# Compression's activation at high priority, a second raw tile loaded ahead, one more sample unit outside the own tiles, and a transpose one output tile later

## The chip, the cores and the metric

The kernel runs on one core of a Trainium2 chip. A core has five engines that work side by side, each through its own queue in order: TensorE (PE: matrix products and transposes; PEld is its weight load), VectorE (DVE), ScalarE (ACT: activation functions, copies), GpSimd (POOL) and SyncE (SP, which here issues DMAs). The metric is the device time of one execution in microseconds. The kernel before took 1641.71 us as the median of three runs (1640.44 to 1644.45).

## The reference

One layer of a decoder trunk for two groups of requests that share the weights: a prompt of 1024 tokens, and eight sample sequences of eight new tokens with 4096 cached ones. In short:

```python
h = rms_norm(x, norm1) * (1 + scale1) + shift1
z = h @ w_in
(q, kc, vc, ks, vs, kw, vw, gates, conv_bg, conv_cg, conv_h, pool_in) = jnp.split(z, IN_SPLITS, axis=-1)
...
k_cmp = rms_norm(compress(full[:, :, 0], cmp_pe[0], cmp_w1[0], cmp_w2[0]), k_gain[0])
v_cmp = compress(full[:, :, 1], cmp_pe[1], cmp_w1[1], cmp_w2[1])
o_cmp, p_cmp = cmp_attention(q, k_cmp, v_cmp, q_pos)
top_i, sel_ok = select_blocks(p_cmp, q_pos, -(-full.shape[1] // SLC_BLOCK))
o_slc = slc_attention(q, top_i, sel_ok, q_pos, full[:, :, 2], full[:, :, 3])
...
o_attn = (g[..., 0:1] * o_cmp + g[..., 1:2] * o_slc + g[..., 2:3] * o_win).reshape(B, T, ATTN_W)
...
x = x + gate1 * (jnp.concatenate([o_attn, y_conv, y_pool], axis=-1) @ w_out)
h = rms_norm(x, norm2) * (1 + scale2) + shift2
x = x + gate2 * swiglu(h, w_up, w_down)
```

The compression, which two of the four edits touch, is this; `raw` is the cache of the raw keys or values of a sequence, read page by page through a page table:

```python
blk = raw[:, idx] + pe[:, None, :]
...
return jax.nn.silu(flat @ w1) @ w2
```

`idx` takes blocks of 32 positions every 16 positions. All data are float32.

## The kernel before

The layer is computed in stages, one after the other, and within a stage several generators ("the attention of the prompt", "the compression", and so on) are run interleaved. Each generator yields the time at which its next step is ready by a planner's own clock (`self.t`, advanced by `self.use`), and the planner takes a ready step. Behind the planner the framework's scheduler orders the instructions on each engine by a priority, that is by their place in the program unless `high_priority(offset=AHEAD)` moves them 2000 places ahead, and by a simulated time at which they are ready. A small edit can therefore move instructions in a whole stage.

The stages on the profile's time: normalisation and input projection up to about 364 us; the attention stage up to about 811; the output projection; then the feed-forward part up to the end.

*Compression.* Each of the eight sample sequences has four raw tiles, numbered 0 to 31 over all, of 128 partitions by 8 pages of 256 numbers. `compress_load(i)` takes a tile from the pool `stream` (three buffers, one of which holds the weights w1 through the stage) and gathers its eight pages with eight DMAs of 128 KB: six on SP's queue and two on POOL's (L533). In `compress`, PE multiplies a tile by w1 in 16 products (`stream` as the input, two rows of the trace for each). Once its products are issued, tile i + 2 is loaded. Two tiles are evacuated together by ACT and DVE (L586 to L590) into `pair` tiles. When a sequence's four tiles are done, `compress_post` adds two of these (L623, DVE), applies Silu (L625, ACT, with a load of its function table), and multiplies by w2 (`pair,c_w` on PE), then normalises. The next sequence may not start its evacuation before `compress_post` has released the pair tiles.

The first EARLY = 3 sequences are compressed during the input projection, with one tile more, number 12, loaded ahead. `compress_more` then compresses the prompt's own keys, for which `compress_prompt` borrows a stream tile. The remaining tiles, 12 to 31, belong to the attention stage. There, before the change, tile 14 went into the buffer that `compress_prompt` had left, and tile 13 into that of tile 12, after its products.

*Prompt attention.* For eight blocks j of queries and two halves h there are two units each, with the selected and compressed keys ("slc") and with the window's ("win"). A unit is: scores on PE as sums of three products of a high and a low part (`kh,qh`, `kl,qh`, `kh,ql`), mask and maximum on DVE (L1136), exponential on ACT (L1148), the scale on DVE (L1150 to L1154) and POOL (L1158), transposes of the probabilities on PE (`ident,P`, L145), their evacuation (`pt`), and the products with the values (`pt,vt`, `pt,vcp`).

*Sample attention.* 36 units, nine for each pair of sequences. Each loads a tile of 1 MB, and does scores (`unit,qb` or `stream,qb`), the exponential (`e`, L1408), four transposes (`ident,e`), their evacuation (`spt`, L163 or L165) and the products with the values (`unit,spt`) into `part`. `sample_load` gives a unit a tile: two tiles `unit` belong to the sample attention alone, and once all the compression is done the three stream tiles join them, but only for units with a number below LATE_UNITS:

```python
fit = [x for x in self.unit_free if self.unit_next < LATE_UNITS or x == "unit"]
```

A pair of sequences ends with `sample_combine`, a chain on DVE (L1458) that weighs eleven parts into `co`. The last pair's `co` is transposed and stored by `sample_store(3)`, which stands in the output projection.

*Output projection.* For each quarter c of the tokens and each of eight output tiles m: 24 products (`mh,w_hi`, `mh,w_lo`, `ml,w_hi`), then the residual (L1517). `mh` and `w_hi` are the high parts of the mixed activations and of the weights, made by ACT at L177, `ml` and `w_lo` the low parts by DVE at L173. The last `sample_store` is issued after the products of c = 0, m = 2.

Of the kernel before, what the change touches and what calls it, by code (L numbers as in the profile page):

```python
# [11 lines left out]
AF = mybir.ActivationFunctionType  # L12
OP = mybir.AluOpType
# [29 lines left out]
AHEAD = 2000  # L43
EARLY = 3
PACE = 0.5
LATE_UNITS = 33
PINNED = ("q3",)
EPS = 1e-6

# [15 lines left out]
class Kernel:  # L65
# [508 lines left out]

    def compress_more(self):
        yield from self.compress_prompt(self.cp)
        self.octets = 0

    def compress_evac(self, uv, vt, pre, half, n=16):
# [40 lines left out]

    def compress_post(self, pool, b, vt, pre, r, w=256):
        nc = self.nc
        nc.vector.tensor_tensor(pre[:, :, 0:w - 1], pre[:, :, 0:w - 1], vt[:, :, 1:w], op=OP.add)  # L623
        r = self.use("dve", 0.1 + w * 0.0023, r)
        nc.scalar.activation(vt[:, :, 0:w], pre[:, :, 0:w], AF.Silu, bias=self.pec[:, 0:1])  # L625
        r = self.use("act", 0.2 + w * 0.002, r, table="silu") + 0.2
        if b is None:
            nc.vector.memset(vt[:, :, w - 1:w], 0.0)
# [17 lines left out]
        r = self.use("act", 0.55, self.t["pe"])  # L646
# [3 lines left out]
        m = yield from self.bank_of(self.cmp_tags[0])  # L650
# [13 lines left out]
        r = self.use("act", 0.4, self.t["pe"], table="sqrt")  # L664
# [3 lines left out]
        r = self.use("dve", 0.1 + w * 0.0077, r)  # L668
# [679 lines left out]
    def sample_load(self, pool):  # L1348
# [4 lines left out]
        while self.unit_next < 36:  # L1353
            fit = [x for x in self.unit_free if self.unit_next < LATE_UNITS or x == "unit"]
            if not fit:
# [193 lines left out]
    def output_projection(self, wp, pool, nt, x1, opened):  # L1549
        nc = self.nc  # L1550
# [57 lines left out]
        for cs in groups:  # L1608
            ss = {c: nt.tile([P, HALF], F32, name="n_ss", bufs=2) for c in cs}
            for m in range(KT):  # L1610
                w = ws.pop(0)
                load()
                for c in cs:
# [7 lines left out]
                    else:  # L1621
                        for k in range(KT):
                            done = self.mm3(acc[:, :HALF], wk[k], parts[c, k][:2], k == 0, k == KT - 1)
                    if c == 0 and m == 2:
                        with self.tc.issue_after(done.ins):
                            self.sample_store(3, self.bank(), self.co, self.smo)
                    if c == cs[-1]:
# [2 lines left out]
                    r = self.residual(xv, acc[:, :HALF], m, c * HALF, HALF, self.mod[:, 2], xv, nt)  # L1630
                    nc.sync.dma_start(self.x1_d[:, m, c * HALF:c * HALF + HALF], xv)
                    r = self.square_sum(nt, ss[c], xv, m, HALF, r, HALF, None)
# [771 lines left out]
```

## Time and profile before

| what | us |
|---|---|
| median of three runs | 1641.71 |
| the profiled execution | 1639.42 |
| its span | 1637.8 |
| PE busy, share of the span | 1557.0, 95% |
| DVE / ACT / POOL busy | 1084.8 / 783.2 / 694.1 |
| PE idle from 364 to 437 us | 16.0 |
| PE idle from 437 to 800 us | 19.6 |
| PE idle from 800 to 828 us | 7.8 |

Times in the profile count from the span's start. A row of a timeline has the start, the length, the engine, the line of the kernel, the operation and its output and inputs by the names of the tiles; "x32" is a count of rows drawn together. What stands in brackets is the time for which the engine was idle just before, and what ended it. In the trace a product of float32 shows as two rows, in the order of the program as one.

### The profile page before, as it was taken

What the parts mean: (1) busy time and instruction counts of PE and PEld (TensorE: products, weight loads), DVE (VectorE), ACT (ScalarE), POOL (GpSimd) and SP (SyncE); (2) the same over time, 40 slices, a digit from 0 to 9 for tenths busy, and PEclk for the clock granted to TensorE, in tenths of its full rate; (3) what the DMA queues carried; (4) which work ended last, traced back from release to release, by engine and by line L of the source; (5) the groups of instructions that cost most, each with busy time, mean ns of one, the idle gap of its engine ahead of it and who ended that gap; (6) DMA issues with size and microseconds to landing.
All of it is one profiled execution on the core that took longest, in us unless ns stands there. A gap on an engine that the chain in (4) does not pass through costs nothing. (4 is left out here: it accounts for less than half of the span.)

```text
span 1637.8 us, 35584 instructions
## 1 busy us (share of the span) xinstructions
PE 1557.0 (95%) x12569; PEld 1378.3 (84%) x12569; DVE 1084.8 (66%) x2660; ACT 783.2 (48%) x1852; POOL 694.1 (42%) x848
## 2 busy tenths in 40 slices
PE   6999999996999999998899999999999999899998
PEld 2899997895777665655599999999999999899998
DVE  4823224895565678765689878777777775577768
ACT  3522215445676766756666534333433443344444
POOL 3231010265243223323213357554554444788765
PEclk9999999997999999999999999999999999999999
DMA  9585665555566475243396864446343445967643
GB/s 341 193 289 173 190 200 156 146 174 167 164 191 184 141 211 156 85 134 107 137 313 217 289 226 177 147 166 212 134 148 136 146 147 198 374 236 253 215 159 126
DMA packets 198020, 309.47 MB, mean 189 GB/s; under 512 B 26513, under 2 KB 132306, under 8 KB 197522
## 3 DMA queue, kind: packets, MB, share of 16 engines
q1 hardware_dynamic: 175346, 268.50, 49.7%
q0 software_dynamic: 9568, 28.40, 5.3%
q10 hardware_dynamic: 12928, 10.29, 2.1%
q8 instruction: 100, 1.64, 0.4%
q14 instruction: 78, 0.64, 0.1%
HBM read 237.10 MB, written 74.20 MB: 190 GB/s over the span
## 5 line engine op out<-in xcount | busy, mean ns | idle before, releaser
L141 PE MATMUL bank<-b_lo,w_hi 128*128 128x272 f32 x1232 | 352.7, 288 | 1.0 <-DVE b_lo L173 1.0
L141 PE MATMUL bank<-b_hi,w_hi 128*128 128x272 f32 x1232 | 350.5, 289 | 2.6 <-ACT f_m L1752 1.2
L141 PE MATMUL bank<-b_hi,w_lo 128*128 128x272 f32 x1232 | 347.3, 288 | 0.0
L141 PEld LDWEIGHTS bank<-b_hi,w_hi 128*128 128x128 f32 x1232 | 229.8, 188 | 5.1 <-ACT f_m L1752 3.0
L141 PEld LDWEIGHTS bank<-b_lo,w_hi 128*128 128x128 f32 x1232 | 231.6, 188 | 2.0 <-DVE b_lo L173 1.9
L141 PEld LDWEIGHTS bank<-b_hi,w_lo 128*128 128x128 f32 x1232 | 229.5, 188 | 0.0
L1158 POOL TENSOR_SCALAR P<-P,st 128x128 f32<-128x128 f32 (+10 forms) x192 | 108.6, 580 | 229.0 <-DVE st L1154 152.0
L173 DVE TENSOR_TENSOR w_lo<-w_raw,w_hi 128x512 fp32r<-128x512 f32 (+2 forms) x118 | 113.6, 972 | 78.7 <-ACT w_hi L177 78.1
L173 POOL TENSOR_TENSOR w_s<-w_raw 128x512 f32<-128x512 f32 (+1 forms) x84 | 119.9, 1428 | 61.9 <-DVE w_lo L173 42.2
L141 PEld LDWEIGHTS bank<-stream 128*128 128x128 f32 x1056 | 125.8, 196 | 17.3 <-issue 10.5
L177 ACT ACTIVATE w_hi<-w_raw 128x512 fp32r<-128x512 f32 (+2 forms) x120 | 79.5, 678 | 125.9 <-PE bank L141 80.2
L141 PE MATMUL bank<-stream 128*128 128x128 f32 x1056 | 132.0, 282 | 6.3 <-DMA stream<-in_cacheA 6.2
L1148 ACT ACTIVATE P<-P,st 128x128 f32<-128x128 f32 (+10 forms) x192 | 112.7, 588 | 52.4 <-DVE st L1136 33.5
L173 POOL TENSOR_TENSOR x<-x,d_m 128x272 f32<-128x272 f32 x136 | 117.5, 886 | 32.7 <-DVE x L1952 18.6
L141 PE MATMUL bank<-h_hi,w_hi 128*128 128x384 f32 (+1 forms) x384 | 130.7, 340 | 0.5 <-DVE q L769 0.5
L141 PE MATMUL bank<-g,w_hi 128*128 128x272 f32 x616 | 121.7, 293 | 6.6 <-DVE x L1952 6.6
L141 PE MATMUL bank<-h_hi,w_lo 128*128 128x384 f32 (+1 forms) x384 | 126.2, 329 | 0.0
L141 PE MATMUL bank<-h_lo,w_hi 128*128 128x384 f32 (+1 forms) x384 | 125.6, 327 | 0.0
L173 DVE TENSOR_TENSOR w_lo<-w_s,w_hi 128x512 fp32r<-128x512 f32 (+1 forms) x119 | 112.4, 946 | 16.8 <-ACT w_hi L177 14.4
L141 PE MATMUL bank<-g,d_hi 128*128 128x272 f32 x616 | 119.0, 289 | 1.3 <-DVE x L1955 1.3
L1779 POOL TENSOR_TENSOR pair<-pair,f_v 128x272 f32<-128x272 f32 x44 | 44.9, 1021 | 174.2 <-DVE f_v L1749 132.4
L1952 DVE SCALAR_TENSOR_TENSOR x<-bank,mod,x 128x272 f32<-128x272 f32 (+1 forms) x200 | 90.4, 476 | 41.2 <-PE bank L141 28.5
(381 smaller groups left out, 3826.6 us busy)
## 6 DMA issues: line engine op xcount, KB each, us to landing
g<-g_d SPq DMA_DIRECT2D x63, 544.0 KB, 6.2
g_d<-f_s SPq DMA_DIRECT2D x57, 544.0 KB, 3.4
wada<-in_wada SPq DMA_DIRECT2D x96, 256.0 KB, 5.4
stream<-in_cacheA SPq DMA_DIRECT2D x192, 128.0 KB, 3.2
unit<-in_cacheB SPq DMA_DIRECT2D x152, 128.0 KB, 2.3
w_raw<-in_wup SPq DMA_DIRECT2D x38, 512.0 KB, 4.3
stream<-in_cacheB SPq DMA_DIRECT2D x104, 128.0 KB, 2.2
w_raw<-in_wout SPq DMA_DIRECT2D x24, 512.0 KB, 5.6
```

The costliest lines, as they stand in the source:

```text
L141: return self.nc.tensor.matmul(out, lhsT, rhs, start=start, stop=stop, skip_group_check=chain)
L173: (self.nc.vector if eng == "dve" else self.nc.gpsimd).tensor_tensor(out, a, b, op=op)
L177: self.last_hi = self.nc.scalar.activation(hi, src, AF.Copy)
L1148: nc.scalar.activation(Ps, Ps, AF.Exp, scale=-1.0, bias=sy[:, g, 0:1], accum_out=sy[:, g, 1:2])
L1158: nc.gpsimd.tensor_scalar(Ps, Ps, sy[:, g, 3:4], 0.0, op0=OP.mult, op1=OP.add)
L1779: nc.gpsimd.tensor_tensor(g[:, 1], s1, v, op=OP.mult)
L1952: self.last_gate = nc.vector.scalar_tensor_tensor(out[:, :n], acc[:, :n], self.mod[:, 5, m, 0:1], out[:, :n], op0=OP.mult, op1=OP.add)
```

## The change

Four edits:

- `compress_more` loads tile 13 (EARLY * 4 + 1) once `compress_prompt` is through.
- In `compress_post` the addition and the Silu stand under `high_priority`.
- LATE_UNITS is 34 and not 33, so that unit 33 may take a stream tile, and only units 34 and 35 are bound to the two tiles `unit`.
- The last `sample_store` is issued after the products of m = 3 and not m = 2.

```diff
-LATE_UNITS = 33
+LATE_UNITS = 34
...
     def compress_more(self):
         yield from self.compress_prompt(self.cp)
+        self.compress_load(EARLY * 4 + 1)
         self.octets = 0
...
     def compress_post(self, pool, b, vt, pre, r, w=256):
         nc = self.nc
-        nc.vector.tensor_tensor(pre[:, :, 0:w - 1], pre[:, :, 0:w - 1], vt[:, :, 1:w], op=OP.add)
-        r = self.use("dve", 0.1 + w * 0.0023, r)
-        nc.scalar.activation(vt[:, :, 0:w], pre[:, :, 0:w], AF.Silu, bias=self.pec[:, 0:1])
+        with self.tc.high_priority(offset=AHEAD):
+            nc.vector.tensor_tensor(pre[:, :, 0:w - 1], pre[:, :, 0:w - 1], vt[:, :, 1:w], op=OP.add)
+            r = self.use("dve", 0.1 + w * 0.0023, r)
+            nc.scalar.activation(vt[:, :, 0:w], pre[:, :, 0:w], AF.Silu, bias=self.pec[:, 0:1])
         r = self.use("act", 0.2 + w * 0.002, r, table="silu") + 0.2
...
-                    if c == 0 and m == 2:
+                    if c == 0 and m == 3:
                         with self.tc.issue_after(done.ins):
                             self.sample_store(3, self.bank(), self.co, self.smo)
```

The order on the engines changes through the whole attention stage. Three places follow. In these rows the number is the row's place on its engine, then come the line, the operation with its tiles, its shape and a count; numbers behind a tile's name only tell its copies apart.

The first is PE at the start of the attention stage, where `stream` is a raw tile of the compression and `kh`, `kl` are the keys of the first prompt unit. Before:

```order
1477 L141 MATMUL bank<-h_sq,mean_h 128x320
1478 L141 MATMUL bank<-stream 128x128 x16
1479 L141 MATMUL bank<-kh_3584,qh 128x192 x4
1480 L141 MATMUL bank<-kh_3586,qh 128x128
1481 L141 MATMUL bank<-kl_3585,qh 128x192 x2
1482 L141 MATMUL bank<-kh_3584,ql 128x192 x2
1483 L141 MATMUL bank<-kl_3585,qh 128x192 x2
1484 L141 MATMUL bank<-kh_3584,ql 128x192 x2
1485 L141 MATMUL bank<-stream 128x128 x14
```

After:

```order
1477 L141 MATMUL bank<-h_sq,mean_h 128x320
1478 L141 MATMUL bank<-stream 128x128 x48
1479 L141 MATMUL bank<-kh_3611,qh 128x192 x2
1480 L141 MATMUL bank<-kl_3612,qh 128x192 x2
1481 L141 MATMUL bank<-kh_3611,ql 128x192 x2
1482 L141 MATMUL bank<-kh_3611,qh 128x192 x2
1483 L141 MATMUL bank<-kl_3612,qh 128x192 x2
1484 L141 MATMUL bank<-kh_3611,ql 128x192 x2
1485 L141 MATMUL bank<-kh_3613,qh 128x128
1486 L141 MATMUL bank<-stream 128x128 x16
```

Before, tile 12 was followed by scores and then by tile 13; now the three tiles 12, 13 and 14 stand in a row, and the scores behind them.

The second is PE in block j = 3, first half, from the last scores with the selected keys to the first transposes of their probabilities (`ident,P`). Before:

```order
1665 L141 MATMUL bank<-kh_3584,ql 128x256 x2
1666 L141 MATMUL bank<-unit,qb 64x512 x2
1667 L145 MATMUL bank<-ident,P 128x64
1668 L141 MATMUL bank<-pt,vt__291 64x256 x4
1669 L145 MATMUL bank<-ident,P 128x64 x7
1670 L141 MATMUL bank<-pair_5299,c_w_82 64x256 x2
1671 L145 MATMUL bank<-ident,e 128x128 x4
1672 L141 MATMUL bank<-stream 128x128 x16
1673 L141 MATMUL bank<-pt,vt__291 64x256 x2
1674 L141 MATMUL bank<-pair_5966,mean_h 128x256
1675 L145 MATMUL bank<-ident,pair_5966 128x128 x2
1676 L145 MATMUL bank<-ident,P 128x64 x32
```

The eight `ident,P` of rows 1667 and 1669 belong to an earlier unit; row 1676 is this unit's. After:

```order
1677 L141 MATMUL bank<-kh_3611,ql 128x256 x2
1678 L141 MATMUL bank<-stream 128x128 x7
1679 L141 MATMUL bank<-unit,spt 64x128 x8
1680 L141 MATMUL bank<-kh_3613,qh 128x512 x2
1681 L141 MATMUL bank<-kl_3614,qh 128x512 x2
1682 L141 MATMUL bank<-kh_3613,ql 128x512 x2
1683 L141 MATMUL bank<-kh_3613,qh 128x512 x2
1684 L141 MATMUL bank<-kl_3614,qh 128x512 x2
1685 L141 MATMUL bank<-kh_3613,ql 128x512 x2
1686 L145 MATMUL bank<-ident,P 128x64 x16
```

A whole raw tile stood between the scores and the transposes; now it is seven products of one, a sample unit's products with its values, and the scores of the window unit.

The third is the end of the attention stage, where `unit,qb`, `ident,e` and `unit,spt` are sample unit 35 and `mh,w_hi` begins the output projection. PE before:

```order
2163 L145 MATMUL bank<-ident,P 63x128 x3
2164 L141 MATMUL bank<-unit,spt 64x128 x8
2165 L141 MATMUL bank<-pt,vt__291 64x256 x2
2166 L141 MATMUL bank<-pt,vcp 64x256 x2
2167 L141 MATMUL bank<-unit,qb 64x512 x2
2168 L145 MATMUL bank<-ident,e 128x128 x4
2169 L141 MATMUL bank<-unit,spt 64x128 x8
```

PE after:

```order
2173 L141 MATMUL bank<-unit,qb 64x512 x2
2174 L141 MATMUL bank<-pt,vt__291 64x256 x2
2175 L141 MATMUL bank<-pt,vcp 64x256 x2
2176 L145 MATMUL bank<-ident,e 128x128 x4
2177 L141 MATMUL bank<-unit,spt 64x128 x8
```

ACT at the same place, from unit 35's exponential (L1408, after the change L1410) to the copy of its transposes, `spt`. Before:

```order
628 L1408 ACTIVATE e,den<-e,nm 128x512
629 L177 ACTIVATE mh<-pair_6564 128x272 x2
630 L177 ACTIVATE mh<-pair_6566 128x272
631 L1447 ACTIVATE cw<-nm,cs 128x2
632 L177 ACTIVATE mh<-pair_6566 128x272
633 L177 ACTIVATE mh<-pair_6568 128x272 x2
634 L177 ACTIVATE mh<-pair_6570 128x272 x2
635 L177 ACTIVATE w_hi<-w_raw 128x512 x2
636 L163 ACTIVATE spt<-bank 128x512
```

After:

```order
619 L1410 ACTIVATE e,den<-e,nm 128x512
620 L177 ACTIVATE mh<-pair_6613 128x272 x2
621 L1230 ACTIVATE mo<-bank 128x256
622 L1449 ACTIVATE cw<-nm,cs 128x2
623 L177 ACTIVATE mh<-pair_6615 128x272 x2
624 L177 ACTIVATE mh<-pair_6617 128x272 x2
625 L177 ACTIVATE mh<-pair_6619 128x272 x2
626 L163 ACTIVATE spt<-bank 128x512
```

On PE, unit 35's scores moved ahead of the last products with the values; on ACT, one copy `mo` stands ahead of `spt` where two `w_hi` stood. The first `part` copy behind `spt` (L163), which stood behind four `w_hi` and six `mh`, now stands behind six `w_hi`.

## The prediction, made before the changed kernel was run

> **What bounds the kernel now.** I read the head of the profile first: busy time of each engine, then the chain that ended last.
>
> ```profile
> span 1637.8 us, 35584 instructions
> PE 1557.0 (95%) x12569; PEld 1378.3 (84%) x12569; DVE 1084.8 (66%) x2660; ACT 783.2 (48%) x1852; POOL 694.1 (42%) x848
> PE 9%; DVE 1%; issue 0%; POOL 0%; ACT 0%; DVEq 0%
> ```
>
> TensorE (PE) works 95% of the span, no other engine over 66%, and the chain is PE's nearly throughout. So this change can win or lose only the time in which PE is idle, or runs at a lower granted clock, in the stretches it reorders. The program's matmuls are the same before and after; only their order differs. The windows by stage say how much idle time there is:
>
> ```profile
> 364.00:437.00 73.00, 57.01 (x468) 46.33 (x466) 42.95 (x204) 39.49 (x131) 35.35 (x84) 0.86 0.58 174
> 437.00:800.00 363.00, 343.37 (x3514) 234.35 (x3516) 234.30 (x985) 239.64 (x629) 109.95 (x182) 0.97 0.49 142
> 800.00:828.00 28.00, 20.20 (x156) 17.03 (x153) 20.12 (x54) 17.15 (x41) 5.01 (x6) 0.94 0.69 243
> 870.00:1638.00 768.00, 748.37 (x5897) 743.01 (x5897) 567.63 (x1022) 328.76 (x736) 445.04 (x431) 0.99 0.56 194
> ```
>
> Columns: start:end, length, busy time (and instructions) of PE, PEld, DVE, ACT and POOL, then the granted clock of PE, DMA share and GB/s. The start of the attention stage (364 to 437) holds 73.00 - 57.01 = 16.0 us of idle PE and a granted clock of 0.86; its middle (437 to 800) 19.6 us; its last units and the first output tiles (800 to 828) 7.8 us. Behind 870 PE is busy and nothing there is touched in kind: whatever is won up to 828 moves the rest earlier, one for one. Two rows of PE's waits in the stage (364 to 870), grouped by what it waited for (total, times, longest), are used below; the waits with a place of their own are shown in the timelines:
>
> ```profile
> PE bank L141 <- ACT kh L177: 1.5, 2, 1.0
> PE bank L145 <- POOL P L1158: 1.8, 2, 1.7
> ```
>
> **The start: load ahead, and Silu at high priority.** PE's timeline, with DVE's, ACT's, SP's and POOL's beside it (start, length, operation; in brackets the idle time before, and what ended it):
>
> ```profile
> 365.39 3.73 PE L141 MATMUL bank<-stream 128*128 128x128 f32 x32
> 374.80 0.53 PE L141 MATMUL bank<-kl,qh 64*128 64x192 f32 x2 [3.41 <-DVE kl L173]
> 380.93 5.88 PE L141 MATMUL bank<-stream 128*128 128x128 f32 x28 [4.96 <-DMA stream<-in_cacheA]
> 392.10 1.00 PE L145 MATMUL bank<-ident,P 64*128 64x64 f32 x12
> 398.20 2.05 PE L141 MATMUL bank<-stream 128*128 128x128 f32 x16
> 403.75 1.02 PE L145 MATMUL bank<-ident,P 128*7 128x128 f32 x4 [1.71 <-DVE st L1150]
> 406.99 1.13 PE L141 MATMUL bank<-pair,c_w 64*64 64x256 f32 x8 [2.21 <-ACT pair L625]
> 408.05 4.80 PE L141 MATMUL bank<-stream 128*128 128x128 f32 x32
> 437.04 0.66 PE L141 MATMUL bank<-pair,c_w 64*64 64x256 f32 x8 [1.24 <-ACT pair L625]
> ...
> 369.16 2.96 SPq L533 DMA_DIRECT2D stream<-in_cacheA  x6
> ...
> 377.88 1.17 POOL L533 DMA_DIRECT2D stream<-in_cacheA  x2 [1.01 <-issue]
> ...
> 403.24 0.29 DVE L590 COPY pair<-bank 64x128 f32<-64x128 f32 x1
> 403.65 0.67 DVE L623 TENSOR_TENSOR pair<-pair,pair 128x510 f32<-128x510 f32 x1
> ...
> 404.92 1.28 ACT L625 ACT_TABLE_LOAD   x1
> 406.21 0.72 ACT L625 ACTIVATE pair<-pair,pec 128x512 f32<-128x512 f32 x1
> ```
>
> A raw tile is 16 matrix products, 32 rows of the trace, 3.73 us. Before, PE takes tile 12 at 365.39, some of the first scores, and then stands till 380.93 for tile 13. That tile goes into tile 12's memory: SP issues six of its eight gathers when tile 12 is done (369.16), but POOL's two come at 377.88, behind the constants that POOL builds. After, tile 13 is in place, and it is tile 14 that goes into tile 12's memory. It is gathered by the same six and two DMAs at the same places of the queues (POOL's two again behind the constants and ahead of kl), so I expect it at the same 380.93. The number of gathers is the same; none is added. What changes is what PE does meanwhile: tile 13 (3.73 us, from 369.1 to 372.9) in place of the 13 score products, and one wait of 8.0 us (380.93 - 372.9) in place of 1.5 (ACT's kh, two waits), 3.41 and 4.96 us.
>
> Onward from 380.93: tile 14 at the low clock, as 28 rows took 5.88 us, ends at about 387.4; first scores 1.2 us (twelve of 192 columns at about 0.1); tile 15 to 392.6 (its memory, tile 13's, is free at 372.9, and POOL's part follows tile 14's with some 8 us to spare); scores of the window branch to 393.5; the first transposes, which wait for the softmax chain (an estimated 0.9 us: none if that chain keeps up) and take 1.00, to 395.4. Then c_w needs the Silu. Before, tile 15 ended at 398.20 + 2.05 = 400.25, its evacuation on DVE at 403.53, and add, table load and Silu led to 406.99. High priority can close the gaps in this only: the add started 0.12 us behind the copy, and ACT was free for the table load 0.60 us behind the add. So the edit itself is worth at most 0.7 us here, and none or little where ACT and DVE are free; its cost, 0.67 us of DVE and 2.0 of ACT ahead of softmax work, is hidden by the same waits. From 392.6, with 3.3 us of evacuation and 2.3 to 2.8 behind it, c_w comes at about 398.2: a wait of 2.7 us (1.1 where the evacuation takes 0.7 as its four copies alone, 3.8 with all the delays of before). For the second c_w I put 2.1 (0.5 to 3.8, the same bounds).
>
> Idle after: 0.5 at the entry, 8.0, 0.9, 2.7, 2.1 = 14.2, against 16.0: **1.8 us won.** Then the clock:
>
> ```profile
> 381.00:384.00 3.00, 3.00 (x14) 3.00 (x15) 2.54 (x27) 2.21 (x13) 0.69 (x2) 0.50 0.00 0
> 403.00:407.00 4.00, 1.03 (x6) 0.39 (x6) 1.70 (x8) 3.97 (x12) 2.10 (x7) 0.53 0.87 271
> 407.00:412.00 5.00, 5.00 (x34) 4.24 (x35) 0.48 (x2) 1.07 (x3) 0.00 (x0) 0.69 0.70 200
> ```
>
> The column ahead of the last two is the granted clock: 0.50 behind the wait at 380.93, which comes after as well, so this loss stays; and 0.53 to 0.69 behind the two waits at 403 to 407. There the transposes took 1.02 us for four (twelve took 1.00 at 392.10: 0.7 lost), c_w 1.13 instead of the 0.66 of 437.04 (0.5 lost), the tile 4.80 instead of 3.73 (1.1 lost), 2.3 in all. After, one wait of 2.7 stands there instead of two close together: I take half of it, 1.15 us, as won, and an estimated 0.6 for the 13 scores between 370 and 376, half of the 1.2 us above, which ran slow behind the waits there (two took 0.53 at 374.80): **1.7 us won**. The start gives 3.5 us, with bounds from -0.4 (both c_w waits 3.8, slow clock as before) to 7.8 (waits 1.1 and 0.5, none for the transposes, no slow clock at c_w).
>
> The Trainium skill speaks to this in "TensorE: Matmul & The Clock Gate", Part 1: the clock falls to one half after an idle window of about 3.4 us and comes back after as long a stretch of work. The row at 381 agrees; the row at 403 does not, where waits of 1.71 and 2.21 us, neither as long, went with 0.53. By the rule alone a single wait of 2.7 us would leave the clock up, and the start would gain 1.15 us more. The Trainium skill's "ScalarE: Activation LUTs", What ACT_TABLE_LOAD costs, puts a drain of 1.38 us on top of a load's 1.28; the rows at 404.92 and 406.21 show the Silu starting 0.01 us behind the load, so by that rule c_w would come 1.4 us later than I say, and the trace speaks against it.
>
> **The middle: a new order, and shorter covers.** From 437 to 800 the scheduler interleaves the same products otherwise. What counts is the PE work that stands between the last scores of a unit (prompt block j, half h) and the transposes of its probabilities P; I call it the cover. Under it DVE, ACT and POOL do the softmax. Counted in the order with the trace's durations of the same shapes, the cover changes from before to after so: (3,0) 8.2 to 5.5 (its rows are shown with the change; 16 raw-tile products, 3.7 us, stood in it before, seven after), (3,1) 6.9 to 5.2 and its window 11.0 to 6.2, (4,0) 9.3 to 6.2, (4,1) 9.3 to 6.1, (5,0) 9.7 to 7.1, (6,0) 9.5 to 5.4; the others stay at 6 or more or grow. How long the softmax takes:
>
> ```profile
> 513.20 0.28 PE L141 MATMUL bank<-kh,ql 64*128 64x256 f32 x2
> 706.39 0.42 PE L141 MATMUL bank<-kh,ql 64*128 64x448 f32 x2
> 716.08 1.21 PE L145 MATMUL bank<-ident,P 64*128 64x64 f32 x32 [1.69 <-POOL P L1158]
> ...
> 519.77 1.36 POOL L1158 TENSOR_SCALAR P<-P,st 128x512 f32<-128x512 f32 x2 [0.16 <-DVE st L1154]
> 714.02 2.00 POOL L1158 TENSOR_SCALAR P<-P,st 128x896 f32<-128x896 f32 x2 [4.33 <-DVE st L1154]
> ```
>
> For (3,0) from 513.48 to 521.13, 7.65 us; for (6,1) from 706.81 to 716.02, 9.2 us, and PE did wait 1.69 there. With 7.65 everywhere the seven would wait 11.9 us in place of 0.8, 11.1 more; with chains that close up to their covers, nothing more. I take 2 us, near the lower end: in 32 units the waits for P sum to 1.8 us, so the chains have so far bent to the cover that the order left them, (3,1)'s 6.9 among them. **2 us lost** (0 to 11).
>
> **The end: unit 33 in a stream tile, the last transpose a tile later.** PE, then ACT:
>
> ```profile
> 801.75 0.60 PE L141 MATMUL bank<-pt,vt__291 128*64 128x256 f32 x4
> 802.28 0.65 PE L141 MATMUL bank<-pt,vcp 63*64 63x256 f32 x4
> 805.59 0.66 PE L145 MATMUL bank<-ident,e 128*128 128x128 f32 x4 [1.65 <-ACT e L1408]
> 809.85 1.98 PE L141 MATMUL bank<-unit,spt 128*64 128x128 f32 x16 [3.61 <-ACT spt L163]
> 816.12 0.39 PE L141 MATMUL bank<-mh,w_hi 128*128 128x272 f32 x1 [0.61 <-ACT part L163]
> 824.32 0.33 PE L145 MATMUL bank<-ident,co 128*128 128x128 f32 x1 [1.93 <-DVE co L1458]
> ...
> 808.18 1.13 ACT L177 ACTIVATE w_hi<-w_raw 128x512 fp32r<-128x512 f32 x2
> 809.22 0.58 ACT L163 ACTIVATE spt<-bank 128x512 f32<-128x512 f32 x1
> ```
>
> Unit 35's scores (unit,qb) now stand ahead of the last pt,vt and pt,vcp, whose 1.2 us then cover the exp: its wait falls from 1.65 to 0.45. The copy of spt leaves ACT's queue with one mo copy (0.38) ahead of it in place of two w_hi (1.13): about 0.65 off the 3.61. Part's copy comes ahead of the mh of the next columns: 0.6 off. The last wait, 1.93 for co, gets the 24 products of one more output tile in front, 3.1 us at the pace of the 48 between 816.12 and the end of work at 824.32 - 1.93 = 822.39; as PE arrives 2.4 us earlier by the savings above and DVE's chain may not, I count 1.4 of it. 1.2 + 0.65 + 0.6 + 1.4 = **3.85 us won** (1.5, if only the reordering of unit 35 and 0.3 of the last wait hold, to 4.4 with all of it). What is late next is the residual at L1517, which follows its own products.
>
> **Sum.** 3.5 - 2 + 3.85 = 5.35 us off the profiled execution of 1639.42 us (span 1637.8): 1634.1. The median of the three runs is 1641.71, 2.3 above that execution; I predict against the median: 1636.4.
>
> **Rivals.**
> (a) *The middle gives most of it back.* A loss of 6 there (softmax 6.8 us) leaves 1.35: 1640.4. For it: seven shorter covers. Against: 1.8 us of such waits so far.
> (b) *Slower.* The softmax of the units of blocks 3 to 6 stays where it was measured, 8.4 us as the mean of 7.65 and 9.2: the seven wait 17.1 in place of 1.7, 15.4 lost, net 8 us: 1649.8. It decides from 12.3 us of loss, a chain of about 7.9.
> (c) *The load ahead does not help.* The long wait merely changes its name, the Silu is as late as ever, clock as before: start -0.4 to 1, the rest 1.85: 1639.5.
> (d) *The start gains all it can*, 7.8: 1632.0.
> The diff does do what it says: the order shows the 48 products in a row and the transpose a tile later.
>
> **How the numbers follow.** A measurement of this kernel can tell about 0.3%, 4.9 us, from no change, so faster is below 1636.8 and slower above 1646.6. Forecast 0.48 (its own range 1632.5 to 1639; 0.34 of it below 1636.8, 0.14 above), (a) 0.14, (b) 0.12, (c) 0.13, (d) 0.13. Faster 0.34 + 0.13 = 0.47; within 0.14 + 0.14 + 0.13 = 0.41, less 0.01 for a larger loss than (a)'s; slower 0.13. The range reaches down to (d) with 2 us for its bounds, 1630, and up past (a) and (c) to 1646; most of (b) stays out.
>
> **What would show it.** Right: one wait of 7 to 8.5 us for stream ahead of about 381, and 48 products of 12 and 13 without a gap before it; first c_w at 397 to 400; no wait at ident,co; idle from 800 on some 4 us less. Wrong: waits of 1 to 3 us for P at the seven units named; a wait at the first c_w over 4; tile 14 landing later than 382.

## The result, and the profile after

| | before | after |
|---|---|---|
| median, us (runs) | 1643.08 (4: 1640.44 to 1645.18) | 1661.07 (4: 1660.9 to 1662.37) |
| the profiled execution, us | 1639.42 | 1662.37 |
| ratio of after to before | | 1.0119 (1.0102 to 1.0135) |

The changed kernel is 18 us slower. The prediction was 1636.4, in a range from 1630 to 1646; it was wrong.

The head of the profile after:

```profile
span 1660.8 us, 35600 instructions
PE 1570.4 (95%) x12569; PEld 1394.3 (84%) x12569; DVE 1086.0 (65%) x2662; ACT 783.6 (47%) x1850; POOL 688.8 (41%) x848
```

PE executes the same 12569 instructions and is busy 13.4 us longer (1570.4 - 1557.0). The rest of the loss is waiting. The attention stage is taken in both traces from the first product of tile 12 to the first product of the output projection (`mh,w_hi`). The windows have the columns explained in the prediction. Before:

```profile
365.39:811.76 446.37, 406.02 (x4033) 283.95 (x4031) 282.58 (x1212) 286.99 (x779) 146.85 (x266) 0.95 0.50 149
811.76:1637.80 826.04, 803.32 (x6323) 796.83 (x6321) 617.49 (x1129) 368.23 (x824) 452.20 (x436) 0.99 0.58 202
```

After, with the first 73 us of the stage by themselves in the first row:

```profile
367.73:440.73 73.00, 56.98 (x455) 49.12 (x454) 38.23 (x180) 38.40 (x122) 35.52 (x84) 0.86 0.55 168
...
369.12:833.08 463.96, 413.77 (x4033) 294.30 (x4031) 282.31 (x1213) 287.41 (x775) 144.55 (x265) 0.94 0.48 143
...
833.08:1660.80 827.72, 805.11 (x6323) 799.03 (x6321) 618.80 (x1130) 368.46 (x826) 449.48 (x437) 0.99 0.58 202
```

Of the 23.0 us between the spans, 3.73 lie ahead of the stage (369.12 - 365.39), 17.59 in it and 1.68 behind it. In the stage PE idles 9.84 us more (463.96 - 413.77 = 50.19 against 40.35) and takes 7.75 us longer for the same 4033 rows: the granted clock is lower. The first row is the stretch of 364 to 437 before, moved on by 3.73: 56.98 busy at a clock of 0.86, against 57.01 at 0.86. The start won nothing.

The 3.73 us ahead of the stage are no effect of the change. Nearly all of them come from a stretch where PE works throughout in both executions, at half the clock in one. After, then before:

```profile
80.00:87.00 7.00, 7.00 (x35) 7.00 (x35) 3.13 (x9) 2.49 (x5) 4.36 (x7) 0.51 1.02 347
```

```profile
80.00:87.00 7.00, 7.00 (x63) 7.00 (x63) 2.59 (x9) 1.98 (x5) 4.69 (x8) 1.00 1.05 379
```

The first experiment below is the changed program instruction for instruction, and its profiled execution shows 1.00 there. Of the sixteen profiled executions of this study, fourteen begin the stage between 368.4 and 369.9, and only that one and the kernel before's at 365.4 to 366.0. Within the stage, too, the slower work varies between executions (a table with the experiments shows how much), and the idle time hardly does.

PE's waits after, in the stage (364 to 870; total, times, longest):

```profile
PE bank L145 <- POOL P L1160: 12.4, 8, 3.1
PE bank L141 <- DMA stream<-in_cacheA: 10.2, 3, 8.4
PE bank L141 <- ACT pair L627: 6.3, 4, 2.9
PE bank L141 <- DMA unit<-in_swinKV: 5.2, 1, 5.2
```

The waits for P went from 1.8 us to 12.4. The raw tiles cost 10.2 in place of 6.2. A wait of 5.2 for a sample unit's load (`in_swinKV`) had no counterpart. The same waits in their places, in PE's timeline after:

```profile
369.12 7.31 PE L141 MATMUL bank<-stream 128*128 128x128 f32 x64
384.87 6.63 PE L141 MATMUL bank<-stream 128*128 128x128 f32 x32 [8.44 <-DMA stream<-in_cacheA]
398.67 0.46 PE L145 MATMUL bank<-ident,P 64*128 64x64 f32 x8 [1.67 <-POOL P L1160]
401.10 1.02 PE L145 MATMUL bank<-ident,P 128*7 128x128 f32 x4 [1.97 <-POOL P L1160]
402.79 1.13 PE L141 MATMUL bank<-pair,c_w 64*64 64x256 f32 x8 [0.67 <-ACT pair L627]
434.12 0.66 PE L141 MATMUL bank<-pair,c_w 64*64 64x256 f32 x8 [1.90 <-ACT pair L627]
...
543.49 0.72 PE L145 MATMUL bank<-ident,P 64*128 64x64 f32 x16 [0.71 <-POOL P L1160]
548.98 0.66 PE L141 MATMUL bank<-pair,c_w 64*64 64x256 f32 x8 [2.92 <-ACT pair L627]
570.54 1.97 PE L141 MATMUL bank<-unit,qb 128*64 128x512 f32 x4 [5.22 <-DMA unit<-in_swinKV]
597.15 1.21 PE L145 MATMUL bank<-ident,P 64*128 64x64 f32 x32 [1.93 <-POOL P L1160]
656.30 1.49 PE L145 MATMUL bank<-ident,P 64*128 64x64 f32 x32 [1.75 <-POOL P L1160]
704.26 0.54 PE L141 MATMUL bank<-kh,ql 64*128 64x448 f32 x2
715.62 1.97 PE L145 MATMUL bank<-ident,P 64*128 64x64 f32 x32 [3.07 <-POOL P L1160]
...
827.68 0.66 PE L145 MATMUL bank<-ident,e 128*128 128x128 f32 x4 [0.64 <-ACT e L1410]
831.17 1.98 PE L141 MATMUL bank<-unit,spt 128*64 128x128 f32 x16 [2.83 <-ACT spt L163]
848.36 0.48 PE L145 MATMUL bank<-ident,co 128*128 128x128 f32 x1 [2.37 <-DVE co L1460]
```

The 64 rows at 369.12 are tiles 12 and 13, in one go as predicted. Behind the long waits the work is slow: tile 14 took 6.63 us, where a tile takes 3.73, and the 32 transposes at 715.62 took 1.97, where the same 32 at 597.15 took 1.21.

### The profile page after: what moved, and what is told of

Read it like the earlier page. It is cut to its first block, busy times and chain, and to the rows that moved or that the text cites. A ratio compares the mean times of both kernels' runs of the same rounds, so it can differ in the third digit from the quotient of the medians.

```text
span 1660.8 us, 35600 instructions
## 1 busy us (share of the span) xinstructions
PE 1570.4 (95%) x12569; PEld 1394.3 (84%) x12569; DVE 1086.0 (65%) x2662; ACT 783.6 (47%) x1850; POOL 688.8 (41%) x848
## 4 chain that ended last, share of the span: by engine, by line
PE 46%; DVE 8%; DMA 3%; ACT 3%; POOL 3%; issue 2%; ACTq 0%; DVEq 0%; POOLq 0%; SPq 0%
PE bank L141 43%; PE bank L145 3%; DVE P L1138 2%; ACT P L1150 1%; DVE w_lo L173 1%; POOL w_s L173 1%; DMA w_raw<-in_wup 1%; DMA w_raw<-in_wout 1%; DVE b_lo L173 1%; DMA x<-x_d 1%; DVE d_lo L173 0%; POOL b_t L173 0%; POOL P L1160 0%; DVE n_ss L173 0%; DVE x L1954 0%
## 5 line engine op out<-in xcount | busy, mean ns | idle before, releaser
L141 PEld LDWEIGHTS bank<-stream 128*128 128x128 f32 x1056 | 131.0, 203 | 22.8 <-issue 19.3
L141 PE MATMUL bank<-stream 128*128 128x128 f32 x1056 | 137.3, 290 | 10.3 <-DMA stream<-in_cacheA 10.2
```

The costliest lines, as they stand in the source:

```text
L141: return self.nc.tensor.matmul(out, lhsT, rhs, start=start, stop=stop, skip_group_check=chain)
```

## The experiments

Of the four edits, the two that stand for the high priority and for LATE_UNITS move nothing: with these two alone, the order of the instructions is that of the kernel before on all five engines; and the changed kernel has the order of the kernel with the other two edits alone. So what is measured belongs to the load ahead and to the later transpose, and the reordering of the stage comes from the load ahead. Each experiment is timed against the kernel before on the same chip; brackets behind a ratio are its 95% interval.

### Which edit

The load ahead together with the later transpose:

```diff
+        self.compress_load(EARLY * 4 + 1)
...
-                    if c == 0 and m == 2:
+                    if c == 0 and m == 3:
```

> The load ahead and the later transpose, without the high priority and with LATE_UNITS at 33. Theory (the load ahead alone reorders the stage, and the other two edits move no instruction): the time of the changed kernel, 1659 to 1663 us, with the same waits. Rival (the priority of the Silu or the rule for the tiles has a part in the loss): clearly less, 1645 to 1655.

Measured: 1656.67 us (4 runs, 1654.11 to 1662.11), ratio 1.0095 (1.0073 to 1.0118), with the waits of the changed kernel to within 0.4 us in each group (P 12.4, raw tiles 10.1, pair 6.0, `in_swinKV` 5.4). The time is a little below the range expected. This is the changed program, so its eight executions in all run from 1654.1 to 1662.4. Between the two of them that were profiled (1654.11 and 1662.37) the difference is slower work and not waiting: 3.17 us ahead of the stage and 4.96 us of PE's busy time in it, with idle times of 50.66 and 50.19.

The load ahead alone (the first line of that diff):

> The load ahead alone. Theory (it is the cause of the loss): 1658 to 1664 us, PE's waits for P and for the window load of a sample unit as in the changed kernel. Rival (the later transpose has a part of the loss at the stage's end, where the wait for co is still 2.4 us): 1650 to 1656.

Measured: 1658.7 us, 1.0082 (1.0056 to 1.0107). As far as the times can tell, the whole loss comes from this one line. At the stage's end it waits longer for `co` than either kernel:

```profile
848.62 0.33 PE L145 MATMUL bank<-ident,co 128*128 128x128 f32 x1 [4.77 <-DVE co L1459]
```

The later transpose alone (the last two lines of that diff):

> The later transpose alone. By the prediction's last term the wait for co (1.93 us before) goes: 1.4 to 1.9 us less, 1640 to 1642, within what a run can tell; PE waits less than 0.3 us at ident,co. Rival (DVE's chain is what is late and follows): the wait stays at 1 us or more and the time is that of before.

Measured: 1641.75 us (10 runs), 0.9997 (0.9985 to 1.0009). The wait for `co`, 1.9 us, is gone. PE's waits from 800 to 940 show what is late next, here and then in the kernel before:

```profile
PE bank L141 <- DVE n_ss L173: 4.4, 2, 2.7
```

```profile
PE bank L141 <- DVE n_ss L173: 2.5, 2, 1.7
```

Another operand from DVE (`n_ss`) is later by what the transpose gave. The same holds in the new order: the load ahead alone waits 4.77 for `co` and 0.20 for `n_ss`, with the later transpose 2.30 and 2.85 (first experiment).

### Is the late load of unit 8 the cause?

The wait of 5.22 at 570.54 is for the load of sample unit 8. On SP's queue after (SPq), that load stands behind 24 gathers of other units, whose issue takes 15 us:

```profile
547.72 15.32 SPq L533 DMA_DIRECT2D stream<-in_cacheB  x24
563.63 0.43 SPq L1371 DMA_DIRECT2D unit<-in_swinKV  x1
```

In the experiment POOL's queue issues this one load; PE's order stays that of the changed kernel:

```diff
-            self.nc.sync.dma_start(kv.rearrange("p (b t) f -> p b t f", b=2),
+            (self.nc.gpsimd if u == 8 else self.nc.sync).dma_start(kv.rearrange("p (b t) f -> p b t f", b=2),
```

> The changed kernel with the window load of sample unit 8 issued by POOL and not by SP; PE's order is the same. Theory (this load is late because SP issues 24 gathers for units 9 to 11 ahead of it): the wait of 5.2 us goes, and with it up to 3.4 us of slow clock: 1652 to 1656 us. Rival (the load waits for its memory, which unit 6 holds): 1659 to 1662 and a wait of 4 us or more.

Measured: 1658.52 us, 1.0089 (1.0072 to 1.0106), a miss. The load was issued 2.1 us earlier only, since POOL itself stood until the unit's memory was free, and other work of POOL stood behind it:

```profile
561.55 0.76 POOL L1371 DMA_DIRECT2D unit<-in_swinKV  x1 [7.24 <-PE bank L141]
```

The wait of 5.2 became 0.3, and these came in its place on PE:

```profile
572.99 1.21 PE L145 MATMUL bank<-ident,P 64*128 64x64 f32 x32 [3.06 <-POOL P L1160]
578.30 1.12 PE L145 MATMUL bank<-ident,e 128*128 128x128 f32 x4 [4.10 <-ACT e L1410]
```

Here POOL's queue, made to wait, handed the delay to the softmax that it serves, and all waits for P rose to 16.4 us. So the run shows that the wait can't be had back this way, and not what the load would be worth if it came early at no cost.

### Are the shorter covers the cause?

The planner allows 1.2 us between the end of a unit's softmax by its own clock and its transposes. More of it puts more work into the cover, less of it shortens the cover. That one number was varied, with the change and without:

```diff
-        self.spawn(0, self.values(pool, u, j, half, br, Pt, seg, ready + 1.2))
+        self.spawn(0, self.values(pool, u, j, half, br, Pt, seg, ready + 3.6))
```

The changed kernel with 3.6:

> The changed kernel with 3.6 in place of 1.2 us of slack in the planner ahead of a prompt unit's transposes, which reorders the stage. Counted as in the prediction, the covers of blocks 3 to 7 lack 1.5 us in all to 7.5 us each (before: 1.5, changed kernel: 11.9). Theory (the loss is the softmax chain of 7.5 us or more under covers shorter than that, and the clock that falls with each wait): the time of before or up to 4 us less, 1638 to 1645, PE's waits for P under 3 us behind block 2. Rival (tile 13's early load costs by itself, by its buffer or by tiles that come too late): 1653 to 1662.

Measured: 1655.91 us, 1.0078 (1.0057 to 1.0098), a miss, inside the range of the rival, which the next section tests. Behind block 2 two waits for P are left, 1.33 and 2.46 us, where the changed kernel has five with 8.3; the theory had put them under 3. But the stage idles 51.8 us, against 50.2 in the changed kernel. Its waits (364 to 930):

```profile
PE bank L141 <- DMA stream<-in_cacheA: 11.1, 2, 8.4
PE bank L145 <- POOL P L1160: 7.4, 4, 2.5
PE bank L141 <- ACT pair L627: 7.0, 4, 3.3
PE bank L141 <- ACT pt L163: 5.3, 8, 2.0
PE bank L145 <- ACT e L1410: 5.2, 5, 2.0
PE bank L141 <- DMA unit<-in_cacheB: 4.0, 4, 1.6
```

So longer covers took away more than half of these waits for P, and other waits took their place.

The changed kernel with 0.6:

> The changed kernel with 0.6 us of that slack and not 1.2; the covers lack 2.9 us. Theory: 1638 to 1648, although the planner leaves less slack. Rival (early load): 1653 to 1662.

Measured: 1654.24 us, 1.0085 (1.006 to 1.0109), a miss, inside the rival's range again; PE still waits 11.8 us for P, in eight places.

The kernel before, no edit, with 0.6; by the count of the prediction its covers then lack 12.4 us of the time that the softmax needs:

> The kernel before, without any of the four edits, with 0.6 us of that slack; the covers lack 12.4 us. Theory: slow like the changed kernel, 1650 to 1662, with 8 us or more of waits for P. Rival (early load is the cause): 1640 to 1647.

Measured: 1657.07 us, 1.0084 (1.0067 to 1.0102), as expected. The waits for P rise from 1.8 to 10.9 us, and one sample chain makes PE wait 8.1 us for `co` at the end of a pair.

The kernel before, no edit, with 2.0; its covers then lack 3.8 us:

> The kernel before with 2.0 us of the planner's slack ahead of the transposes; none of the four edits. The covers of blocks 3 to 7 lack 3.8 us to 7.5. Theory (any other order than the one that the constants were set for has some 10 us more of waits, wherever they fall): 1650 to 1660. Rival (the covers alone count): 1643 to 1648.

Measured: 1659.35 us, 1.0099 (1.0081 to 1.0117), as expected. Here the covers lack little, and the kernel is as slow as the changed one. The window of its attention stage:

```profile
369.57:837.49 467.92, 408.49 (x4032) 286.05 (x4031) 287.99 (x1215) 288.03 (x785) 147.75 (x267) 0.94 0.48 145
```

59.4 us idle in a stage of 467.92. Its waits for P are 5.7 us; 5.8 are for the very load of `in_swinKV` that the change made late, 6.9 for `e`, 10.4 for raw tiles. So an order that nobody meant to change, moved by one constant of the planner, costs what the change costs, and by the same kinds of waits.

### The early load with the order kept

If the order is what costs, the early load itself should be free. First, what the late raw tile is worth: in the kernel before, SP issues all eight gathers of tile 13 and none stands behind POOL's constants; PE's order changes within block 0 only:

```diff
-            self.raw[i] = (t, self.gather(t, "cacheA", i // 4, i % 4 * 8, 8, 2))
+            self.raw[i] = (t, self.gather(t, "cacheA", i // 4, i % 4 * 8, 8, 0 if i == 13 else 2))
```

> The kernel before with all eight gathers of tile 13 on SP, none on POOL; the order behind block 0 is that of before. Theory of the start (the tile comes late because POOL issues its share behind the constants): the wait for it falls from 5 us to under 1.5, and 3 to 6 us are won, 1637 to 1640. Rival (the first softmax waits for POOL's kl in any case, and gives it back at the first transposes): 1641 to 1644.

Measured: 1638.93 us (10 runs), 0.998 (0.9966 to 0.9994), as expected; the tile's wait went from 4.96 to 0.93:

```profile
380.95 5.02 PE L141 MATMUL bank<-stream 128*128 128x128 f32 x28 [0.93 <-DMA stream<-in_cacheA]
```

Second, the load ahead with the planner's clocks put back, so that it plans as if the tile came at its old time; PE's order in the stage behind the first block is then the old one:

```diff
         yield from self.compress_prompt(self.cp)
+        kept = dict(self.t)
+        self.early = self.stream_tile()
+        self.gather(self.early, "cacheA", EARLY, 8, 8, 2)
+        self.t.update(kept)
...
+            if i == EARLY * 4 + 1:
+                r = self.use("pool", 2 * 1.04, self.t["pe"])
+                self.raw[i] = (self.early, max(r, self.use("dma", 6 * 0.5, self.t["pe"])) + 2.5)
+                return
```

> The kernel before with tile 13 loaded ahead as in the change, but its planner is told the times of the late load, so that the order behind block 0 stays that of before. Theory (the load is worth some us at the start, and the new order of the rest is what costs): the wait of 5 us for a raw tile falls under 2, 2 to 7 us less than before, 1635 to 1640. Rival (the early load costs by itself): 1650 or more. Second rival (the wait for the tile turns into a wait for the softmax or for POOL's kl): 1641 to 1644.

Measured: 1641.52 us (11 runs), 0.9993 (0.9984 to 1.0002). The load ahead costs nothing here. It also wins nothing, as the second rival had it: the raw tile's wait is gone, and the first scores wait in its place.

```profile
382.14 0.44 PE L141 MATMUL bank<-kh,qh 64*128 64x128 f32 x1 [2.57 <-DVE pair L598]
385.15 0.47 PE L141 MATMUL bank<-kl,qh 64*128 64x128 f32 x2 [2.56 <-POOL kl L173]
```

Third, both: the load ahead in the old order, and tile 14's eight gathers on SP (the same three lines for i == 14, with the gather's last argument 0):

> As the kernel with kept times, and all eight gathers of tile 14 on SP, so that none stands behind POOL's constants. Theory: no wait for a raw tile over 1 us up to 400 us, and 1 to 3 us less than with kept times alone. Rival (POOL's kl, which the first softmax waits for, sets the start now): the same time as with kept times alone, within 1 us.

Measured: 1636.21 us (5 runs, 1634.82 to 1638.18), 0.9965 (0.9952 to 0.9979), faster than both kernels, and 5.3 us below the run before it, more than expected. The start (73 us, as above), and its whole stage:

```profile
367.30:440.30 73.00, 63.52 (x508) 51.44 (x507) 43.07 (x208) 43.99 (x139) 35.03 (x83) 0.86 0.58 178
368.74:808.51 439.77, 405.69 (x4032) 285.09 (x4030) 281.51 (x1212) 287.62 (x780) 145.97 (x264) 0.95 0.51 152
```

PE works 63.52 of the first 73 us, against 57.01 before, and the stage is 6.6 us shorter. So the start can gain what the prediction hoped for, but with the old order and with tile 14's gathers off POOL's queue, and the change has neither. With the later transpose in addition:

> As the one before, with the later last transpose of the change. From the transpose alone (1641.75 against 1642.93): within 1.5 us of the one before; the wait at ident,co gone, and 1.5 to 2 us more waiting for n_ss behind it.

Measured: 1636.17 us, 0.9961 (0.9947 to 0.9974): no difference, since the wait of 2.0 for `co` goes and the one for `n_ss` grows from 1.4 to 2.7.

### What the long wait costs

Two experiments on the changed kernel, PE's order in the stage otherwise untouched. In the first, tile 13's 16 products are done three times over, with the planner's clocks put back, so that PE works while tile 14 loads:

```diff
+                    if i == 13:
+                        kept = dict(self.t)
+                        for _ in range(2):
+                            for kv in range(2):
+                                for k in range(KT):
+                                    self.mm(uv[:, kv, q * 128:(q + 1) * 128], self.w1[:, kv * KT + k, :], rv[:, kv, k],
+                                            k == 0, k == KT - 1)
+                        self.t.update(kept)
```

> The changed kernel with tile 13's 16 products done three times and not once (the same result each time), so that PE works through 7.5 of the 8.4 us for which it waits for tile 14; the rest of its order is that of the change. It does more work, and the wait ends when it did. Theory (a wait costs twice, once as idle time and again by the half clock behind it): the granted clock stays at 1 over tile 14 and the first scores, tile 14's products take 3.7 to 4.5 us and not 6.6, first c_w 2 to 4 us earlier against the front's end, and 2 to 6 us off the changed kernel's time, 1652 to 1659. Rival (the softmax sets the start, so that the faster products only wait longer): the waits for P at the first transposes grow by as much, and the time is the changed kernel's, 1656 to 1662.

Measured: 1652.16 us (5 runs, 1650.02 to 1654.37), 1.0054 (1.004 to 1.0069). PE does 7.1 us more work (14.45 against 7.31) and the kernel is about 4.5 us faster than the same program without it in the first experiment (1656.67), and 9 faster than in the first comparison (1661.07); a part of either difference can be the clock ahead of the stage. The timeline and a window behind the wait, then the same window of the changed kernel:

```profile
369.09 14.45 PE L141 MATMUL bank<-stream 128*128 128x128 f32 x128
384.70 3.81 PE L141 MATMUL bank<-stream 128*128 128x128 f32 x32 [1.16 <-DMA stream<-in_cacheA]
384.00:391.00 7.00, 5.45 (x51) 5.25 (x52) 2.80 (x23) 3.46 (x13) 3.52 (x6) 1.00 0.70 199
```

```profile
384.00:391.00 7.00, 6.13 (x29) 6.16 (x30) 0.00 (x0) 0.00 (x0) 2.44 (x4) 0.51 0.13 39
```

Tile 14 comes at the same time, but its products take 3.81 us at full clock in place of 6.63 at 0.51.

In the second, SP issues all eight gathers of tile 14 (the diff of the first experiment of the last group, with 14):

> The changed kernel with all eight gathers of tile 14 on SP; PE's order is that of the change through the stage. Theory (POOL's two gathers behind its constants make the long wait): the wait of 8.4 us falls to 3 to 5 and the time by 3 to 6 us, 1651 to 1658. Rival (the gathers of SP end as late): no change, 1656 to 1662.

Measured: 1650.8 us, 1.0049 (1.0032 to 1.0066). The wait falls from 8.44 to 4.26 us, and the kernel gains 6 to 10 us, more than the wait itself:

```profile
380.26 5.18 PE L141 MATMUL bank<-stream 128*128 128x128 f32 x32 [4.26 <-DMA stream<-in_cacheA]
```

### The stage in all profiled executions

From the first product of tile 12 to the first of the output projection, in us:

| kernel | length | PE busy | PE idle |
|---|---|---|---|
| before | 446.37 | 406.02 | 40.35 |
| later transpose alone | 449.34 | 409.13 | 40.21 |
| before, tile 13 on SP | 441.03 | 402.35 | 38.68 |
| load ahead, old order | 443.99 | 404.71 | 39.28 |
| the same, tile 14 on SP | 439.77 | 405.69 | 34.08 |
| the same, transpose later | 440.95 | 406.37 | 34.58 |
| after | 463.96 | 413.77 | 50.19 |
| the same program again (first experiment) | 459.47 | 408.81 | 50.66 |
| load ahead alone | 464.06 | 413.03 | 51.03 |
| after, unit 8 on POOL | 461.55 | 410.61 | 50.94 |
| after, allowance 3.6 | 466.52 | 414.71 | 51.81 |
| after, allowance 0.6 | 449.75 | 406.86 | 42.89 |
| before, allowance 0.6 | 459.81 | 412.26 | 47.55 |
| before, allowance 2.0 | 467.92 | 408.49 | 59.43 |
| after, wait filled | 457.81 | 414.75 | 43.06 |
| after, tile 14 on SP | 450.37 | 405.12 | 45.25 |

The old order idles 34 to 40 us, the new one 50 to 51 in four executions. The time for the same products is 402.35 to 409.13 in the old order and 408.81 to 413.77 in those four: the middles of the two ranges lie 5.6 us apart, and their ends overlap. What the last two experiments won lies in the start and in the pace of the work: from 71.6 us behind the first product of tile 12 on, PE idles 24.9 us in the kernel before, 26.0 and 25.1 in the old order with the load ahead (without and with tile 14 on SP), and in the new order 34.7, 34.9 and 35.2 (after, the same program again, load ahead alone), 34.4 with the wait filled and 34.2 with tile 14 on SP. Behind the start the new order has some 10 us more of idle time, whatever is done about the long wait.

## Why the prediction was wrong

**The parts that held.** One wait of 8.0 us ahead of 381 was predicted: 8.44, ending at 384.87, which is 381.1 less the later start. The queues decide that landing, as the prediction said: with POOL's two gathers taken out it moved. The sum at the end stayed within its bounds: `e`, `spt`, `part` and `co` cost 7.8 us before and 5.84 after (0.64 + 2.83 + 2.37), about 2.0 won where 3.85 was predicted and 1.5 was the lower bound. The first three came as predicted (1.01, 0.78 and 0.61 won). The part at fault is the last wait: it was to fall by 1.4 us and rose from 1.93 to 2.37. The later transpose did take 2.5 us off it (4.77 with the load ahead alone, 2.30 with both), but in the new order PE waits longer for DVE's `co`, and what is late next is `n_ss`, where the prediction named the residual. The 1.4 was a choice in any case: with 3.1 us more work ahead and PE 2.4 us earlier, a chain of DVE that stays in its place leaves 0.7. That the order there came from LATE_UNITS, as the part's heading had it, is false: that edit moves nothing.

**The start was mis-sized: 3.5 us predicted, nothing measured.** Its idle time was to fall from 16.0 us to 14.2 and is 16.0 again (73.00 - 56.98). The first transposes wait 1.67 and 1.97 us (0.9 predicted); c_w waits 0.67 and 1.90 (2.7 and 2.1 predicted). The first c_w comes at 402.79, or 399.1 less the later start, where 398.2 was predicted. The saving on the clock, 1.7 us, did not come: the transposes and c_w ran as slowly as before (1.02 and 1.13 us), and the tile behind the long wait took 6.63. The prediction counted that slow tile as a loss that stays, and the long wait as no worse than the three that it replaced. Filling the wait and halving it, in the last two experiments, won 4 to 10 us. So the start went as in rival (c): the long wait merely changed its name.

**The middle failed: 2 us lost predicted, 11.6 us of idle time measured** (the stage's 9.84, and the 1.8 that `e` and `spt` at its end gave back). The step that failed is the one on which the term was chosen: "the chains have so far bent to the cover that the order left them". Of the units named they did in (3,0), with a wait of 0.71 us. They did not in (4,0), (5,0) and (6,0), whose waits are those at 597.15, 656.30 and 715.62. In (3,1) and (4,1) another wait of PE stands just ahead of the transposes, so that none of their own shows (5.22 for unit 8's load, 2.31 for a sample unit's `spt`); with unit 8's load on POOL, (3,1) waited 3.06. Unit (6,0) shows why. Its last scores end at 704.80 (704.26 + 0.54), its transposes begin at 715.62: a chain of 10.8 us, longer than any that the prediction measured. On DVE the scale of this unit stands behind the masks and maxima of the window unit, whose scores now follow directly, and of a sample unit (L1403):

```profile
711.05 0.48 DVE L1138 CUSTOM_DVE_ANT_0 P<-bank,m_edge 128x320 f32<-128x320 f32 x1
...
711.69 0.69 DVE L1403 CUSTOM_DVE_ANT_1 e<-bank,bias 128x512 f32<-128x512 f32 x1 [0.16 <-PE bank L141]
712.31 0.16 DVE L1152 RECIPROCAL st<-st 128x2 f32<-128x2 f32 x1
...
713.57 3.55 POOL L1160 TENSOR_SCALAR P<-P,st 128x896 f32<-128x896 f32 x4 [1.27 <-DVE st L1152]
```

ACT ends the unit's last exponential at 710.67, and the reciprocal that needs it starts at 712.31; the product behind that starts at 713.25, after 0.8 us more of the sample unit's work. By these rows an estimated 2.4 us of the wait of 3.07 is other units' work on DVE. This cover, made of another unit's scores, brought its own softmax work onto the same engines; the prediction counted its PE time and not that. With all waits for P from 500 on at 8.3 us (0.71 + 1.93 + 1.75 + 3.07 + 0.81), against 1.8, this term alone is 6.5, the size of rival (a). Rival (b), 1649.8, came nearest in time, but by 15.4 us of such waits, of which there were 6.5.

The rest was not priced at all. Three things were missing. The load of unit 8 came 5.22 us late; it stands behind 24 gathers on SP, and the order of SP's queue was not followed, though the queue is only a part of it (with POOL's queue the issue came 2.1 us earlier). The wait for the third c_w, 2.92, was not foreseen. And in the middle each wait was priced once, as idle time, though the prediction's own windows show the clock at half around such waits. In the profiled execution of after there are 7.75 us of slower work beside 9.84 of idle time, in the first experiment's 2.8 (408.81 - 406.02); since the executions in the old order differ by nearly 7 us among themselves, how much of it belongs to the waits is open. The Trainium skill's "TensorE: Matmul & The Clock Gate", Part 1, has the clock fall after an idle window of about 3.4 us. The wait of 8.44 and the 0.51 behind it agree; the window from 403 to 407 in the prediction, 0.53 with waits of 1.71 and 2.21 us, and the 1.97 us for transposes behind a wait of 3.07 show that shorter ones can cost it as well. Not each one does: behind 1.93 us, at 597.15, the transposes took their usual 1.21.

**What the experiments settle.** The load ahead alone has the loss. The same load with the planner told the old times costs nothing. With tile 14's gathers on SP the two orders can be compared once more: 1650.8 us in the new one, 1636.21 in the old one, 14.6 us apart, where the load ahead alone in both orders gives 17.2 (1658.7 and 1641.52). The two allowances in the kernel before bring the loss without any edit. So the loss is the price of the new order of the stage, which the load ahead sets off since it changes the planner's clocks. It is not one wait that could be mended: the run with unit 8's load on POOL and the one with the allowance of 3.6 each took away one kind, and others took its place; halving the long wait at the start won 6 to 10 us and left 8.7 (1650.8 against 1642.12). Nor do the covers alone give the time: by the count in the expectations they lack 1.5 us in the kernel before and in the changed one with 3.6, 2.9 with 0.6, and 3.8 in the kernel before with 2.0, and the last three are 11 to 17 us slower than the first.

**What stays open.** Why the old order is better than the others by 11 to 18 us is not known: the five other orders that were run all lost, and no single mechanism was shown. With 0.6, the changed kernel idled 42.89 us in its profiled execution, 2.5 more than before, and its median is 11.5 us above that of the kernel before; that execution was its fastest (1650.19), so how waits and clock share that loss is not known. No run separates the clock from the waits in the middle of the stage; repeating tile 13's products does so at the start only.

## What to carry to other kernels

Where a planner or a scheduler sets the order, a moved load is two changes, the transfer and a new order of everything behind it; put the planner's clocks back and the two can be measured apart (here 0.9993 against 1.0082, and 0.9965 with a queue made free as well). A forecast that counts covers in a new order must also count what else the covering work puts on the engines of the chain, and follow each DMA queue past the moved steps. Price a wait of PE by its length and, where the granted clock falls, by the slow work behind it too.

## What was unexpected of the hardware

- The granted clock differs between executions of one program where the profile shows PE busy throughout. Ahead of the stretch at 80 us PE does products of two columns; afterwards the clock was 0.51 in one execution and 1.00 in the other. That these products are the reason is not shown. The products in the changed kernel, whose window is shown above, then the window in the first experiment, which is the same program:

```profile
77.80 4.17 PE L141 MATMUL bank<-c_peT,stream 128*128 128x2 f32 x29
```

```profile
80.00:87.00 7.00, 7.00 (x65) 7.00 (x64) 2.92 (x9) 2.39 (x5) 4.96 (x8) 1.00 1.02 342
```

- Work that is thrown away can pay: the 32 products of two repetitions in a wait of 8.4 us brought the next tile from 6.63 to 3.81 us and the kernel from 1656.67 or more to 1652.16.
